# Encoder layer on one core: first MLP operands built inside the loop, last group added to the rows directly, row sums of the last chunk made later

## Chip, cores and metric

One core of a Trainium2 chip runs the whole program. The metric is the device time of one execution in microseconds. Engines are named as in the profile: PE (TensorE), DVE (VectorE), ACT (ScalarE), POOL (GpSimd), SP (SyncE, which only issues transfers here).

## What is computed

Two requests (2048 and 256 rows of width 1024) go through one layer: a normalised input projection, three mixers (windowed attention, a Fourier mix, attention into a memory), an output projection with a residual add, and a squared-ReLU MLP of width 4096 with a second residual add and a final norm. The change touches what begins at the output projection:

```python
x = x + group_output_norm(y_attn, y_four, y_mem, g_grp) @ w_out
hf = rmsnorm(x, g_ffn) @ w_ff1
x = x + jnp.square(jax.nn.relu(hf)) @ w_ff2
return rmsnorm(x, g_final)
```

## The kernel before

Rows are handled in 18 blocks of 128. Every fp32 operand of a product is split into a high part (ACT, `hi_of`) and a low part (`lo_of`, on DVE or POOL), and a product is three matmuls.

**Attention stage.** While attention runs, each finished block `b` goes through `outproj(b)`: a generator whose matmuls are drained a few at a time between attention's. It adds the projection to the rows `xr`, writes them to `X2d`, gets the row scale `xst` (squares on ACT, two small instructions on POOL), scales the rows (L845), transposes them in two halves (`xp`, PE) and multiplies by the gain (L855). `keep` (L861) then writes pieces of the result, `Xn`, that the MLP will read.

**MLP.** Rows are handled in three chunks of six blocks. Both products are done with seven half-size products instead of eight (a Strassen-like scheme), so sums and differences of the operands' quarters are needed. For the rows these are made block by block by POOL (L872): the second three blocks of a chunk are combined with the first three, which are fetched back from `XnT`. For chunk `c`, operand `i` of the rows is loaded as `XTl` (L991) and split by `build_x` into `XTh`, `XTl`.

One loop over `n` then interleaves, 14 steps apart, `product(n)` (first product: chunk, column pair `j`, operand `i` in the order `ORD1`) and `half_step(r)` (second product: chunk, group `g` of two column pairs, operand `i` in the order `ORD2`, half `e`). Weights are loaded in granules and split; in the first chunk the split first weights `w1s` (three buffers) are also written to `W1D` for the later chunks; for the second weights ACT makes `w2h` and POOL `w2l` (two buffers each). Each second product gathers in a PSUM tile `y` and DVE adds it to an accumulator `acc`, one per operand and block. After the last group of a chunk `finish(c, i)` combines the accumulators into the output rows (some sums on POOL, some on DVE), `measure` squares them (ACT), and `write` scales and stores them.

**Order.** The program is written in the order above, but a scheduler then orders the instructions of each engine; each engine runs its own list strictly in that order, and so does SP's queue of transfers. Before the loop the program writes the loads and the fourteen split pairs of the first chunk, drains the rest of the output projections of blocks 16 and 17, and frees their memory.

## Time and profile before

| | |
|---|---|
| median of 3 runs | 2377.63 us (2376.19 to 2380.34) |
| profiled execution | 2377.28 us, of which the span is 2375.5 us |
| busy | PE 2229.7 us (94%), DVE 1593.7 (67%), ACT 1003.9 (42%), POOL 1167.2 (49%) |
| chain that ended last | PE 52%, DVE 4%, POOL 3% of the span |

The share of PE is an average over stages. From about 380 to 852 us attention runs, from 922 to 2351 the MLP loop; PE's idle time lies mostly at the start, between these two stages, and at the end.

### The profile page before, as it was taken

How to read it: one execution, taken by the hardware profiler on the slowest of the kernel's cores; microseconds unless marked ns; L12 is line 12 of the kernel's file. 1: busy time of each engine (PE TensorE's matmuls, PEld its weight loads, DVE VectorE, ACT ScalarE, POOL GpSimd, SP SyncE). 2: the span in 40 equal slices, each digit the busy share in tenths (PEclk: the TensorE clock that was granted, in tenths of full speed). 3: DMA queues.
4: the chain of work that ended last, by engine and by line, in shares of the span. 5: the costliest groups of instructions: out<-in, count | busy, mean ns of one | idle time of the engine just before them, and what ended most of it. 6: DMA issues, size and time to landing. Idle time of an engine off the chain costs nothing.

```text
span 2375.5 us, 35784 instructions
## 1 busy us (share of the span) xinstructions
PE 2229.7 (94%) x12464; PEld 2004.1 (84%) x12464; DVE 1593.7 (67%) x2760; ACT 1003.9 (42%) x2353; POOL 1167.2 (49%) x1074
## 2 busy tenths in 40 slices
PE   7999996999998968999999999999999999999994
PEld 7999995887887857899999888999998889999983
DVE  6333477777676765888999986555557765555566
ACT  6332367665665643544444434222224332222233
POOL 3563031124123254877777575444444755444458
PEclk9999998999999988999999999999999999999997
DMA  8986257335444367666666867555557675555542
GB/s 295 322 286 236 93 157 284 128 130 167 150 149 146 125 234 267 243 224 221 226 225 223 314 203 259 193 192 186 188 193 271 205 243 189 192 187 188 195 155 84
DMA packets 187915, 484.89 MB, mean 204 GB/s; under 512 B 19607, under 2 KB 43159, under 8 KB 185431
## 3 DMA queue, kind: packets, MB, share of 16 engines
q1 hardware_dynamic: 168848, 427.20, 53.2%
q0 software_dynamic: 11696, 45.76, 5.7%
q10 hardware_dynamic: 7191, 9.65, 1.2%
q8 instruction: 99, 1.62, 0.3%
q14 instruction: 81, 0.66, 0.1%
HBM read 340.19 MB, written 143.26 MB: 204 GB/s over the span
## 4 chain that ended last, share of the span: by engine, by line
PE 52%; DVE 4%; POOL 3%; issue 1%; DMA 1%; ACT 0%; SPq 0%; POOLq 0%; ACTq 0%; DVEq 0%
PE y L100 26%; PE pc L100 8%; PE pb L100 7%; PE pa L100 7%; PE pd L100 4%; DVE acc L323 1%; POOL w2l L106 1%; DVE XTl L106 1%; DMA w1s<-W1D 0%; DVE al L106 0%; DVE x L323 0%; POOL ms L983 0%; DMA XTl<-Xn 0%; DVE m L323 0%; DVE acc L1194 0%
## 5 line engine op out<-in xcount | busy, mean ns | idle before, releaser
L106 POOL TENSOR_TENSOR w2l<-w,w2h 128x512 fp32r<-128x512 f32 x336 | 476.0, 1418 | 530.8 <-ACT w2h L103 520.5
L100 PE MATMUL y<-w2l,ah 128*128 128x512 f32 x1008 | 397.7, 394 | 13.7 <-POOL w2l L106 13.7
L100 PE MATMUL y<-w2h,al 128*128 128x512 f32 x1008 | 396.9, 395 | 0.0
L100 PE MATMUL y<-w2h,ah 128*128 128x512 f32 x1008 | 374.7, 395 | 6.1 <-DVE acc L323 4.3
L103 ACT ACTIVATE ah<-m 128x384 fp32r<-128x384 f32 x240 | 125.4, 524 | 471.7 <-PE y L100 453.8
L106 DVE TENSOR_TENSOR al<-m,ah 128x384 fp32r<-128x384 f32 x240 | 174.8, 729 | 157.7 <-ACT ah L103 154.3
L323 DVE TENSOR_TENSOR acc<-acc,y 128x512 f32<-128x512 f32 x396 | 255.5, 679 | 28.0 <-PE y L100 25.1
L100 PEld LDWEIGHTS y<-w2l,ah 128*128 128x128 f32 x1008 | 190.2, 189 | 42.3 <-POOL w2l L106 19.9
L100 PE MATMUL pc<-XTh,w1s 128*128 128x384 f32 x768 | 218.7, 339 | 6.9 <-DMA w1s<-W1D 3.2
L100 PEld LDWEIGHTS y<-w2h,ah 128*128 128x128 f32 x1008 | 189.3, 188 | 36.2 <-DVE acc L323 8.8
L100 PEld LDWEIGHTS y<-w2h,al 128*128 128x128 f32 x1008 | 190.1, 189 | 34.4
L100 PE MATMUL pb<-XTh,w1s 128*128 128x384 f32 x768 | 215.8, 337 | 1.5 <-ACT w1s L103 1.5
L100 PE MATMUL pa<-XTh,w1s 128*128 128x384 f32 x768 | 214.7, 338 | 2.0 <-ACT m L1085 1.1
L103 ACT ACTIVATE w2h<-w 128x512 fp32r<-128x512 f32 x336 | 207.2, 617 | 9.9 <-POOL w2l L106 4.4
L100 PE MATMUL pj<-hl_x,winh 128*128 128x256 f32 x720 | 206.6, 289 | 0.0
L100 PE MATMUL pj<-hh_x,winl 128*128 128x256 f32 x720 | 205.6, 287 | 0.0
L100 PE MATMUL pj<-hh_x,winh 128*128 128x256 f32 x720 | 204.1, 289 | 1.3 <-ACT hh_x L103 1.3
L1064 DVE SCALAR_TENSOR_TENSOR m<-m 128x384 f32<-128x384 f32 x192 | 175.5, 914 | 40.6 <-ACT m L1091 37.2
L100 PEld LDWEIGHTS pc<-XTh,w1s 128*128 128x128 f32 x768 | 142.6, 189 | 17.0 <-DVE m L323 3.3
L103 ACT ACTIVATE ah<-ms 128x384 fp32r<-128x384 f32 x96 | 50.5, 526 | 249.5 <-PE y L100 149.4
L100 PEld LDWEIGHTS pa<-XTh,w1s 128*128 128x128 f32 x768 | 142.2, 189 | 9.9 <-ACT m L1085 1.5
L100 PEld LDWEIGHTS pb<-XTh,w1s 128*128 128x128 f32 x768 | 141.9, 189 | 9.2 <-ACT w1s L103 1.9
(234 smaller groups left out, 5249.3 us busy)
## 6 DMA issues: line engine op xcount, KB each, us to landing
w1s<-W1D SPq DMA_DIRECT2D x224, 512.0 KB, 3.5
W1D<-w1s SPq DMA_DIRECT2D x112, 512.0 KB, 4.0
w<-in_w_dram SPq DMA_DIRECT2D x208, 256.0 KB, 3.9
w<-W2T SPq DMA_DIRECT2D x192, 256.0 KB, 3.7
w2r<-in_w_dram SPq DMA_DIRECT2D x16, 1024.0 KB, 7.3
W2T<-w2r POOLq DMA_DIRECT2D x16, 1024.0 KB, 6.2
XTl<-Xn SPq DMA_DIRECT2D x21, 768.0 KB, 8.1
qb<-Qd SPq DMA_DIRECT2D x18, 768.0 KB, 6.9
```

The source lines that it names most:

```text
L100: pe.matmul(out, lhsT, rhs, start=start, stop=stop, skip_group_check=more)
L103: act.activation(out, src, AF.Copy, scale=scale)
L106: (eng or dve).tensor_tensor(out=out, in0=src, in1=hi.bitcast(F32), op=ALU.subtract)
L323: TT(out=o, in0=a, in1=b, op=ALU.add)
L1064: dve.scalar_tensor_tensor(out=r, in0=r, scalar=0.0, in1=r, op0=ALU.max, op1=ALU.mult)
```

## The change

1. `outproj` scales each half of the rows by itself before its transposes, and takes the transposes' PSUM tile always from the same one-buffer pool. `keep` writes by SP's queue instead of POOL's, except for the four sums.
2. For the last chunk `outproj` makes no sums: it writes the second blocks to `XnT`, and a new `late_rows(t)`, called three times in the loop's second chunk, loads four pieces, makes the four sums on POOL and writes them.
3. Blocks 16 and 17 are drained before the MLP's operands are loaded in the program's text; only operands 1 and 6 are built before the loop, the other five in its first five steps, two ahead of their products.
4. `ORD2` runs operand 4 later (1, 2, 5, 6, 7, 4, 3). In the last chunk `finish` combines the accumulators one group earlier, and the last group uses `last_half_step`: products that go to the same rows gather in one PSUM tile, and each result is added to the rows directly.
5. In the last writes ACT scales the half whose gain POOL has multiplied already.

```diff
             rstd_of_means(st)
-            dve.tensor_scalar(out=xt, in0=xt, scalar1=st[:, 0:1], scalar2=None, op0=ALU.mult)
             xv = xt.rearrange("p (n t) -> p n t", n=2)
             for n in range(2):
...
+                dve.tensor_scalar(out=xv[:, n], in0=xv[:, n], scalar1=st[:, 0:1], scalar2=None, op0=ALU.mult)
+                ps = ps_p.tile([P, 4, P], F32, tag="p", name=f"xp_{b}_{n}")
...
-            def keep(i, v):
-                pool.dma_start(Xn[c, i][:, :, r * P:(r + 1) * P], v.rearrange("p (k t) -> p k t", k=KT // 2))
+            def keep(i, v, eng=sp):
+                eng.dma_start(Xn[c, i][:, :, r * P:(r + 1) * P], v.rearrange("p (k t) -> p k t", k=KT // 2))
...
+                if c == NCH - 1:
+                    sp.dma_start(XnT[b], xt)
+                else:
...
-        ORD2 = (1, 2, 4, 5, 6, 7, 3)
+        ORD2 = (1, 2, 5, 6, 7, 4, 3)
...
+        def last_half_step(r):
...
+                if e == 1:
+                    if i == 1 or i == 2:
+                        add(A(2, t), A(2, t), ps)
+                    elif i == 5:
+                        add(A("x", t), A("x", t), ps)
+                    elif i == 6 or i == 3:
+                        add(A(3, t), A(3, t), ps)
+                    elif i == 7:
+                        add(A("x", t), A("x", t), ps)
+                        add(A(4, t), A(4, t), ps)
+                    else:
+                        sub(A(4, t), A(4, t), ps)
...
+            if last_group(c, g):
+                for t in range(NT):
+                    if i == 2:
+                        measure(c, t, 0, A(2, t))
+                        ptt(A(2, t), A(2, t), acc[c, "g"][0], ALU.mult)
...
+        def late_rows(t):
+            a, b = (XnT[(NCH - 1) * CT + o + t].rearrange("p (n t) -> p n t", n=2) for o in (0, NT))
+            g = [granule(f"xl{i}_{t}", s) for i, s in enumerate((a[:, 0], a[:, 1], b[:, 0], b[:, 1]))]
+            for i, o in row_sums(*g):
+                sp.dma_start(Xn[NCH - 1, i][:, :, t * P:(t + 1) * P], o.rearrange("p (k t) -> p k t", k=KH))
...
-        for n, i in enumerate(ORD1):
-            for k in (0, 2):
-                drain(8)
-                build_x(0, i, k)
...
         drain(10 ** 9)
...
+        for n in range(2):
+            for k in (0, 2):
+                build_x(0, ORD1[n], k)
+            operand1(n)
...
+            if 2 <= n + 2 < 7:
+                for k in (0, 2):
+                    build_x(0, ORD1[n + 2], k)
+            if n >= PER + 40 and (n - PER - 40) % 8 == 0 and (n - PER - 40) // 8 < NT:
+                late_rows((n - PER - 40) // 8)
...
-                if g == NG - 1 and e == 1:
-                    pending += finish(c, i)
+                if g >= NG - 1 - (c == NCH - 1) and e == 1:
+                    pending += finish(c, g, i)
```

How the scheduler then orders the engines, at the three places that matter below. First DVE at the passage to the MLP, before the change (block 16's rows are `xr_9965`, block 17's `xr_10279`):

```order
L106 TENSOR_TENSOR XTl_0_10245<-XTl_0_10245,XTh_0_10244 128x768 x2
L323 TENSOR_TENSOR xr_10279<-xr_10279,op_1_10313 128x512
L106 TENSOR_TENSOR XTl_0_10248<-XTl_0_10248,XTh_0_10247 128x768 x2
L106 TENSOR_TENSOR XTl_0_10251<-XTl_0_10251,XTh_0_10250 128x768 x2
L106 TENSOR_TENSOR XTl_0_10254<-XTl_0_10254,XTh_0_10253 128x768 x2
L106 TENSOR_TENSOR XTl_0_10257<-XTl_0_10257,XTh_0_10256 128x768 x2
L106 TENSOR_TENSOR XTl_0_10260<-XTl_0_10260,XTh_0_10259 128x768 x2
L106 TENSOR_TENSOR XTl_0_10263<-XTl_0_10263,XTh_0_10262 128x768 x2
L845 TENSOR_SCALAR xr_10279<-xr_10279,xst_10355 128x1024
L855 TENSOR_TENSOR xr_10279<-xp_0_10363,gain 128x512
L855 TENSOR_TENSOR xr_10279<-xp_1_10369,gain 128x512
```

All seven split pairs stand here, block 17's second residual add behind the first of them and its scaling (L845) behind the last. After the change (block 16 is `xr_9972`, block 17 `xr_10249`):

```order
L323 TENSOR_TENSOR xr_10249<-xr_10249,op_0_10251 128x512
L106 TENSOR_TENSOR XTl_0_10356<-XTl_0_10356,XTh_0_10355 128x768 x2
L106 TENSOR_TENSOR XTl_0_10359<-XTl_0_10359,XTh_0_10358 128x768 x2
L323 TENSOR_TENSOR xr_10249<-xr_10249,op_1_10277 128x512
L106 TENSOR_TENSOR XTl_0_10362<-XTl_0_10362,XTh_0_10361 128x768 x2
L106 TENSOR_TENSOR XTl_0_10365<-XTl_0_10365,XTh_0_10364 128x768 x2
L106 TENSOR_TENSOR XTl_0_10368<-XTl_0_10368,XTh_0_10367 128x768 x2
L106 TENSOR_TENSOR w1s_0_7_10426<-w_0_2_10343,w1s_0_7_10426 128x512
L853 TENSOR_SCALAR xr_9972<-xr_9972,xst_10110 128x512 x2
L858 TENSOR_TENSOR xr_9972<-xp_0_10118,gain 128x512
L106 TENSOR_TENSOR w1s_0_5_10450<-w1s_0_10370,w1s_0_5_10450 128x512
```

Two pairs stand further ahead, not shown. The splits still stand ahead of the scaling, and now block 16's scaling (L853, two halves) is behind them as well; the two residual adds of block 17 stand between the splits. On PE at the same place, before:

```order
L100 MATMUL op_1_10313<-wol_4464,yth_1_10097 128x512
L100 MATMUL op_1_10313<-woh_4463,ytl_1_10098 128x512
L853 MATMUL xp_0_10363<-ident,xr_10279 128x128 x4
L853 MATMUL xp_1_10369<-ident,xr_10279 128x128 x4
L100 MATMUL pa_0_10432<-XTh_0_10244,w1s_0_1_10347 128x384
L100 MATMUL pa_0_10432<-XTl_0_10245,w1s_0_1_10347 128x384
```

Block 17's transposes `xp` follow its last output matmul, and the MLP's first product `pa` stands behind them. After:

```order
L100 MATMUL pb_0_10430<-XTh_0_10352,w1s_0_6_10387 128x384 x2
L100 MATMUL pb_0_10430<-XTl_0_10353,w1s_0_6_10387 128x384
L100 MATMUL pb_0_10430<-XTh_0_10352,w1s_0_6_10387 128x384
L856 MATMUL xp_0_10118<-ident,xr_9972 128x128 x4
L856 MATMUL xp_1_10125<-ident,xr_9972 128x128 x4
L100 MATMUL pc_0_10504<-XTh_0_10361,w1s_0_5_10450 128x384
```

The first two products of the MLP (`pa`, not shown, and `pb`) now stand ahead of block 16's transposes, and block 17's follow one product later. Last, POOL in the last group, before (`acc` and `x` rows are sums of accumulators):

```order
L106 TENSOR_TENSOR w2l_7_2_1_24214<-w_2_7_2_1_24153,w2h_7_2_1_24213 128x512
L106 TENSOR_TENSOR w2l_7_4_0_24236<-w_2_7_4_0_24189,w2h_7_4_0_24235 128x512
L983 TENSOR_TENSOR acc_2_0_20224<-acc_2_0_20224,acc_2_0_20362 128x512
L983 TENSOR_TENSOR acc_2_1_20226<-acc_2_1_20226,acc_2_1_20367 128x512
L106 TENSOR_TENSOR w2l_7_4_1_24261<-w_2_7_4_1_24211,w2h_7_4_1_24260 128x512
L983 TENSOR_TENSOR acc_2_2_20228<-acc_2_2_20228,acc_2_2_20372 128x512
L983 TENSOR_TENSOR ms_14_24243<-ms_14_24243,m_2_14_23746 128x384
L106 TENSOR_TENSOR w2l_7_5_0_24298<-w_2_7_5_0_24233,w2h_7_5_0_24297 128x512
```

After:

```order
L106 TENSOR_TENSOR w2l_7_2_1_24286<-w_2_7_2_1_24219,w2h_7_2_1_24285 128x512
L987 TENSOR_TENSOR ms_14_24268<-ms_14_24268,m_2_14_23795 128x384
L987 TENSOR_TENSOR m_2_14_23835<-m_2_14_23835,ms_14_24268 128x384
L987 TENSOR_TENSOR acc_2_0_20263<-acc_2_0_20263,gf_2_24308 128x512
L987 TENSOR_TENSOR acc_2_1_20265<-acc_2_1_20265,gf_2_24308 128x512
L106 TENSOR_TENSOR w2l_7_5_0_24315<-w_2_7_5_0_24258,w2h_7_5_0_24314 128x512
L987 TENSOR_TENSOR ms_15_24293<-ms_15_24293,m_2_15_24078 128x384
L106 TENSOR_TENSOR w2l_7_5_1_24338<-w_2_7_5_1_24283,w2h_7_5_1_24337 128x512
```

The sums of accumulators are gone from the last group; between operand 2's and operand 5's `w2l` stand now, beside two sums of the operand (`ms`, `m`), two multiplications of rows by the final gain (`gf`), which wait for ACT's measuring of those rows.

## Rows read from the trace of the kernel before

**Rows 1.** PE, DVE, ACT and POOL by stage: each row is a stretch of the span in us, its length, then busy us of each engine with its number of instructions, the granted TensorE clock as a share of 2.4 GHz, the busy share of the DMA engines and GB/s. The stretches are the passage from attention to the MLP, the MLP's first chunk, the last group's second products, and what follows the last matmul.

```profile
852.00:922.00 70.00, 40.85 (x180) 34.99 (x179) 37.90 (x40) 21.21 (x36) 38.91 (x38) 0.78 0.74 268
922.00:1400.00 478.00, 473.21 (x2378) 428.45 (x2377) 418.68 (x530) 207.72 (x389) 335.45 (x238) 1.00 0.70 242
2310.00:2351.00 41.00, 34.44 (x126) 23.66 (x124) 26.90 (x36) 14.82 (x31) 38.56 (x30) 0.96 0.21 58
2351.00:2376.00 25.00, 0.26 (x2) 0.00 (x0) 18.51 (x21) 8.56 (x21) 15.94 (x17) 0.58 0.34 126
```

**Rows 2.** What TensorE waited for, whole span (total us, times, longest): the wait of the block transposes `xp` for the normalised rows `xr`.

```profile
PE xp L853 <- DVE xr L845: 29.4, 5, 22.9
```

**Rows 3.** The passage in order of time, engine by engine (start, us, engine, line, operation, xcount; in brackets the idle time before it and its releaser). First TensorE, from block 16's first output half to the first of the MLP's second products (`y`).

```profile
852.25 0.39 PE L100 MATMUL op<-woh,ytl 128*128 128x512 f32 x1
871.98 0.39 PE L100 MATMUL op<-woh,ytl 128*128 128x512 f32 x1
895.30 1.94 PE L853 MATMUL xp<-ident,xr 128*128 128x128 f32 x8 [22.93 <-DVE xr L845]
898.11 0.66 PE L100 MATMUL pa<-XTh,w1s 128*128 128x384 f32 x1 [0.88 <-DVE xr L855]
911.14 0.69 PE L100 MATMUL pd<-XTh,w1s 128*128 128x384 f32 x1 [2.33 <-ACT w1s L103]
918.41 0.33 PE L100 MATMUL pb<-XTh,w1s 128*128 128x384 f32 x1
920.49 0.33 PE L100 MATMUL pa<-XTh,w1s 128*128 128x384 f32 x1
922.57 0.84 PE L100 MATMUL y<-w2h,ah 128*128 128x512 f32 x3
```

**Rows 4.** The same stretch on VectorE: block 17's second residual add, twelve of the fourteen splits of the first chunk's operands, and block 17's scaling.

```profile
877.48 0.67 DVE L323 TENSOR_TENSOR xr<-xr,op 128x512 f32<-128x512 f32 x1
878.07 14.99 DVE L106 TENSOR_TENSOR XTl<-XTl,XTh 128x768 fp32r<-128x768 f32 x12
892.99 2.16 DVE L845 TENSOR_SCALAR xr<-xr,xst 128x1024 f32<-128x1024 f32 x1
```

**Rows 5.** The same stretch on GpSimd (the power that ends block 17's row scale) and on SyncE's queue (issue of the seven operand loads).

```profile
882.05 1.30 POOL L138 TENSOR_TENSOR xst<-xst,mhalf 128x1 f32<-128x1 f32 x1
864.19 4.60 SPq L991 DMA_DIRECT2D XTl<-Xn  x7
```

**Rows 6.** The instructions on the operand tiles `XTl`, whole span (ns: min/median/max, then first and last start): ScalarE's high part and VectorE's low part.

```profile
L103 ACT ACTIVATE XTh<-XTl x42: 825/830/850, 872.3 to 1838.8; 128x768 fp32r<-128x768 f32 x42
L106 DVE TENSOR_TENSOR XTl<-XTl,XTh x42: 943/950/2242, 874.5 to 1843.6; 128x768 fp32r<-128x768 f32 x42
```

**Rows 7.** Two stretches of 2 us after the long wait, columns as in rows 1.

```profile
912.00:914.00 2.00, 2.00 (x8) 2.00 (x8) 0.00 (x0) 0.00 (x0) 0.00 (x0) 0.50 1.03 348
914.00:916.00 2.00, 1.05 (x5) 0.73 (x3) 0.20 (x1) 0.86 (x2) 0.00 (x0) 0.88 0.50 156
```

**Rows 8.** The end of the first chunk, 20 us stretches, columns as in rows 1; and GpSimd's subtractions that make the row sums, whole span (ns: min/median/max).

```profile
1380.00:1400.00 20.00, 20.00 (x104) 18.24 (x103) 16.10 (x22) 5.69 (x11) 16.64 (x13) 1.00 0.64 204
1400.00:1420.00 20.00, 18.49 (x93) 16.24 (x91) 17.02 (x21) 7.91 (x20) 14.45 (x12) 1.00 0.77 245
1420.00:1440.00 20.00, 16.96 (x81) 14.37 (x81) 20.00 (x25) 7.24 (x18) 17.44 (x18) 1.00 0.77 241
L872 POOL TENSOR_TENSOR xq<-xr,xq x18: 1272/1336/1986, 521.5 to 909.0; 128x512 f32<-128x512 f32 x18
```

**Rows 9.** The last group. GpSimd by line and operation from 2310 to 2351 (xcount, busy us, mean ns of one, idle before), and what TensorE waited for from 2310 on.

```profile
L106 POOL TENSOR_TENSOR w2l<-w,w2h 128x512 fp32r<-128x512 f32 x13 | 18.9, 1456 | 2.4 <-ACT w2h L103 2.4
L983 POOL TENSOR_TENSOR acc<-acc,acc 128x512 f32<-128x512 f32 x8 | 11.7, 1475 | 0.0
L983 POOL TENSOR_TENSOR x<-x,acc 128x512 f32<-128x512 f32 x3 | 4.1, 1390 | 0.0
PE y L100 <- POOL w2l L106: 5.3, 6, 1.3
PE y L100 <- ACT w2h L103: 0.9, 4, 0.3
```

**Rows 10.** The tail in order of time: TensorE's last matmul, four VectorE rows behind it, ScalarE's last instruction.

```profile
2350.87 0.39 PE L100 MATMUL y<-w2h,al 128*128 128x512 f32 x1
2357.26 0.68 DVE L323 TENSOR_TENSOR x<-x,acc 128x512 f32<-128x512 f32 x1
2362.66 1.75 DVE L1194 SCALAR_TENSOR_TENSOR x<-x,ff,gf 128x512 f32<-128x512 f32 x1
2365.59 0.74 DVE L1194 SCALAR_TENSOR_TENSOR x<-x,ff,gf 128x512 f32<-128x512 f32 x1
2370.35 0.75 DVE L1194 SCALAR_TENSOR_TENSOR acc<-acc,ff,gf 128x512 f32<-128x512 f32 x1 [0.84 <-POOL ff L138]
2371.57 0.72 ACT L1192 ACTIVATE acc<-fg,ff 128x512 f32<-128x512 f32 x1 [3.16 <-DVE acc L1194]
```

**Rows 11.** What SyncE's queue waited for, whole span (total us, times, longest), the two rows of the loads of the residual rows `xr`; and who waited for writers of `xr` between 380 and 920.

```profile
SPq L819 <- DMA Xn<-xq: 68.5, 8, 14.0
SPq L819 <- DMA XnT<-xr: 62.0, 5, 16.3
  POOL Xn L861: 36.3, 34
```

More of the change, by code (lines that the diff above doesn't have):

```diff
@@ L814, in open_out, with row_sums @@
                 scaled_split(*wo[k], s, gain[:, 2, k:k + 1])
+        def row_sums(b11, b21, b12, b22):
+            for o, u, v, i in ((b11, b12, b11, 5), (b12, b22, b12, 7), (b22, b22, b11, 6), (b21, b22, b21, 4)):
+                pool.tensor_tensor(out=o, in0=u, in1=v, op=ALU.subtract)
+                yield i, o
         def outproj(B):
@@ L1150, in load_acc, with last_group, multiply @@
                         sp.dma_start(acc[c, i, t], X2d[b][:, n * 512:(n + 1) * 512])
+        def last_group(c, g):
+            return c == NCH - 1 and g == NG - 1
+        def multiply(ps, k, t, start, stop, more=False):
+            ah, al = opsA[k]
+            wh, wl = ops2[k]
+            ts_ = slice(t * P, (t + 1) * P)
+            mm(ps, ah[:, ts_], wh, start, False, more)
+            mm(ps, ah[:, ts_], wl, False, False, more)
+            mm(ps, al[:, ts_], wh, False, stop, more)
         def half_step(r):
             c, g, i, e = steps2[r]
-            ah, al = opsA.pop(steps2[r])
-            wh, wl = ops2.pop(steps2[r])
             for t in range(NT):
@@ L1188, in write @@
                 o = hv[n]
-                if end and n == 1:
-                    t = granule(f"fg_{b}", None)
-                    pool.tensor_tensor(out=t, in0=o, in1=gf[n], op=ALU.mult)
-                    act.activation(o, t, AF.Copy, scale=st[:, 0:1])
+                if end and n == 0:
+                    act.activation(o, o, AF.Copy, scale=st[:, 0:1])
                 else:
@@ L1232, in trunk @@
[L1232 to L1242 removed]
+            if i == 1 and g == NG - 1:
+                acc[c, "g"] = gains_of(c)
+            if last_group(c, g):
+                for t in range(NT):
+                    if i == 2:
+                        measure(c, t, 0, A(2, t))
+                        ptt(A(2, t), A(2, t), acc[c, "g"][0], ALU.mult)
+                    elif i == 7:
+                        measure(c, NT + t, 1, A("x", t))
+                    elif i == 4:
+                        measure(c, NT + t, 0, A(4, t))
+            else:
+                for t in range(NT):
+                    if i == 1:
+                        acc[c, "x", t] = granule(f"x22_{c}_{t}", X2d[c * CT + NT + t][:, 512:1024])
+                    elif i == 2:
+                        ptt(A(2, t), A(2, t), A(1, t), ALU.add)
+                    elif i == 5:
+                        ptt(A("x", t), A("x", t), A(5, t), ALU.add)
+                    elif i == 6:
+                        ptt(A(6, t), A(6, t), A(1, t), ALU.add)
+                    elif i == 7:
+                        add(A(7, t), A(7, t), A(6, t))
+                        ptt(A(6, t), A(6, t), A(5, t), ALU.add)
+                        add(A("x", t), A("x", t), A(7, t))
+                    elif i == 4:
+                        add(A(4, t), A(4, t), A(7, t))
+                    elif i == 3:
+                        add(A(3, t), A(3, t), A(6, t))
+                    if not last:
+                        for o, h, k in ((2, 0, 2), (7, 1, "x"), (4, 1, 4), (3, 0, 3)):
+                            if i == o:
+                                measure(c, h * NT + t, 1 if k in ("x", 3) else 0, A(k, t))
@@ new lines, in finish @@
+            if g == NG - 1 and i == 4:
+                return [lambda t=t: write(c, NT + t, [A(4, t), A("x", t)], acc[c, "g"]) for t in range(NT)]
+            if g == NG - 1 and i == 3 and not last:
+                return [lambda t=t: write(c, t, [A(2, t), A(3, t)], acc[c, "g"]) for t in range(NT)]
+            return []
+        def late_rows(t):
[3 more added lines that the diff above has]
+                sp.dma_start(Xn[NCH - 1, i][:, :, t * P:(t + 1) * P], o.rearrange("p (k t) -> p k t", k=KH))
@@ L1246, in trunk @@
         rp = region(right, "right", "ffn_r")
+        ps_y = region(right, "right", "ps_fy", 1, PSUM)
         ps_h = region(right, "right", "ps_fh", 1, PSUM)
-        ps_y = region(right, "right", "ps_fy", 1, PSUM)
+        w1_first(0)
+        for i in ORD1:
+            load_x(0, i)
+        w1_sums(0, 0)
+        for n in range(2):
+            for k in (0, 2):
+                build_x(0, ORD1[n], k)
+            operand1(n)
         w1_first(1)
```

80 lines of the change are left out of this document (27 added, 53 removed).

## Prediction

> **What bounds the kernel now.** I read the stages first, then the waits of TensorE, then the two places where the stages lose time. In the first chunk of the MLP PE is busy 473.2 of 478 us [rows 1]: there, time is saved only by less matmul work, and the change takes none away. The passage from attention to the MLP is another matter: PE works 40.9 of 70 us, at a mean clock of 0.78. Behind the last matmul 24 us pass without PE, and in the last group PE works 34.4 of 41 us while POOL is busy 38.6 [rows 1]. So the three places hold some 29, 24 and 7 us of idle PE, and a low clock beside.
>
> The list of waits names the first: of 29.4 us in which transposes `xp` waited for scaled rows, 22.9 are one wait [rows 2]. In order of time the reader sees it whole: PE ends block 17's output product at 872, starts its transposes at 895.3, and the MLP's first product `pa` stands in the queue behind them until 898.1 [rows 3]. The row scale was there at 883.4, but DVE was in the middle of twelve splits in a row and took up the scaling only at 893.0 [rows 4, 5]. PE was not waiting for the MLP's data; it was waiting, in its fixed order, for an instruction behind other work on DVE.
>
> **The passage (-22 us).** By the order of the changed program PE goes from block 17's output product straight to `pa` and `pb`, with block 16's transposes behind these. PE reached the end of that product at 872 with block 16's transposes (8, under 1 us) already done, so in the new order it gets there near 871. `pa` can start then if its operands are split. The operand loads were issued at 864.2 behind block 16's rows [rows 5]; in the new order they stand ahead of these in SP's queue, so I take them as there. That would be 27 us earlier than 898.1, the upper end.
>
> But the splits are not moved out of the way. DVE's new list has three pairs behind block 17's second add, and block 16's scaling behind these. From the add, which ends near 872: six splits at between 0.95 [rows 6] and 1.25 us (14.99 over 12, rows 4), say 6.4; one low part of a weight and a half scaling, about 1.1. So block 16's transposes start near 879.5. PE has `pa` and `pb` until then, 2.08 us each at full clock (918.41 to 920.49, rows 3), that is until 875.2: a new wait of 4 to 5 us takes the place of the 22.9.
>
> From there to the first second product `y` PE has 16 transposes (2 us), five products (10.4), two waits of about 1.5 for the second halves, since the transposes now share one PSUM buffer, and the wait for weights that it has now (2.33 before `pd`, rows 3), because the three `w1s` buffers turn no faster. That is 18 us at full clock. After a wait of 2.33 us the clock stood at 0.50 for 2 us and at 0.88 for the next 2 [rows 7], at 0.5 of 2.4 GHz the lower level, 1.2 GHz; I put 2 to 3 us on that. `y` then starts near 900 instead of 922.6: -22. Lower bound: if all five products run at 1.2 GHz, 10 us more, -12. Upper: -27.
>
> **The row sums of the last chunk (+4 us).** Twelve subtractions leave this passage, where POOL had them on the way to the row scale, and turn up, by POOL's order, at the end of the first chunk and the start of the second. At 1.34 us each [rows 8] they are 16.1 us of POOL. The three stretches there have POOL busy 48.5 of 60, and PE idle in the last two (1.5 and 3.0 us, rows 8): 16.1 go into 11.5 free, so 4.6 push `w2l` back, and PE with it. Bounds 0 (spread wider) and 16.1. Their 24 transfers lie on a queue whose DMA engines are at 0.64 to 0.77 there; I give them nothing.
>
> DVE is busy 53.1 of the same 60 us, 20 of the last 20 [rows 8]. A DVE instruction with two operands took 0.74 or 1.75 us in the tail, the longer one while POOL ran [rows 10]; 12 times the difference is 12 us, below the upper bound.
> The Trainium skill speaks against the move here: "SBUF — State Buffer", section "Who interferes with whom", has a DVE instruction with two SBUF inputs and a GpSimd instruction that reads SBUF exclude each other for a whole instruction. By that rule each of the twelve can cost DVE its length, which would make this term +12 rather than +4.
>
> **The last group (-2 us).** Eleven sums of accumulators, 15.8 us of POOL, go [rows 9]; they are made one group earlier, where PE has first products to run beside. PE waited 6.2 us for split weights here, and the mean clock was 0.96 of 41 us, 1.6 us [rows 1, 9]. But the two multiplications by the gain now stand ahead of operand 5's `w2l`, and wait for ACT's measuring. From the last matmul of block 1's rows: an add 0.68, the measuring about 0.7, two multiplications and one `w2l` at 1.46 to 1.48: 5.8 us, against nine matmuls, 2.1 us. That is a wait of 3.7, and the third multiplication gives one of about 1.5. So 7.8 becomes some 5.5. Bounds -6.5 (POOL keeps ahead) and +3.
>
> **The tail (-12.7 us).** Behind its last matmul, which ends at 2351.3, the old program has DVE adds of accumulators until 2357.9 and later, nine scalings, some of them stretched from 0.74 to 1.75 us by POOL's work, and ends with ACT at 2372.3, 3.2 us before the end of the span [rows 10]. In the new one DVE has three adds (0.68) and nine scalings (0.74) left, 8.7 us, about 8 since neighbours overlap, with nothing large on POOL; the scales for the first are made while PE ends. With 0.3 us behind them and the same 3.2 us for the transfer: 11.5 instead of 24.2. Bounds -10 (four instructions stretched by 1 us, start half a microsecond late) and -14.5.
>
> **Attention (-2 us).** The other four waits for the scaling are 6.5 us [rows 2]; with halves of half the length, and POOL rid of 51 issues of transfers (counted in the code; 39 go to SP, twelve of the rest to the later sums), I take a third of it. Bounds -6.5 and +9. The other order of `ORD2` changes no count of anything; its operand 5 has its sums one to two steps earlier, and I see no wait there: 0.
>
> **Sum.** 2377.3 (profiled execution; 0.35 below the median) - 22 + 4 - 2 - 12.7 - 2 = 2342.6, on the median 2343.
>
> **Rivals.**
> 1. *The wait stays on DVE* (2353 to 2372, 0.20). The splits are still ahead of the scaling, and if one runs at its longest, 2.24 us [rows 6], or the loads come as late as now (issued at 864), `pa` itself waits and block 16's transposes start near 890. Then the passage gives 10 instead of 22, and with +8 for the row sums the time is 2359. For it: DVE's order. Against: SP's order. (If only DVE is held up by the twelve subtractions, +12 instead of +4, the time is 2351, inside the forecast.)
> 2. *More is won* (below 2331, 0.10). No wait at `xp` (-27), the sums hidden (0), the last group free of waits (-6.5): 2329.
> 3. *SP's queue holds attention back* (0.06). It now carries the 39 writes of normalised rows, and each waits for DVE in front of the loads of the next queries. POOL waited 36.3 us for such rows [rows 11]. If 35 us of these waits reach PE, about 2.2 for each of 16 blocks, all is lost; at 50, 2392, slower. It decides where a load lands after PE has ended the block before it. Against it: the queue stood 68.5 and 62.0 us behind loads that waited for POOL's writes [rows 11], and these get shorter.
> 4. *Nothing moves* (0.02): each wait reappears as another at the same place, 2376.
>
> **How the numbers follow.** The forecast (2331 to 2352) has 0.62. Within 0.2%, 4.8 us, a measurement of this kernel cannot tell a change. Faster by more: the forecast, rivals 1 and 2, 0.92. Same: rival 4 and a third of rival 3, 0.04. Slower: the rest of rival 3, 0.04. The range 2328 to 2366 takes in the forecast, half of rival 2 and some two thirds of rival 1, 0.8.
>
> **What would show it.** Between the end of block 17's output product and `y` there should be 26 to 30 us instead of 50, with one wait of 4 to 5 us at `xp` and its releaser the scaling in halves. The part behind the last matmul should be 11 to 13 us, and the last DVE scaling 4 us or less before the end. In the last group a wait of `y` for `w2h` or `w2l` right behind operand 2. At the first chunk's end POOL over 90% busy. It is wrong if `pa` waits for `XTh` or `w1s` at 871, if attention's stretch gets longer by more than 5 us, or if the end of chunk 1 loses more than 16.

## The result, and the profile after

The changed kernel takes 2342.98 us (median of 4 runs, 2337.87 to 2346.21) against 2376.91 of the kernel before on the same chip: ratio 0.9859 (95% interval 0.9843 to 0.9875), 33.5 us less by the ratio. The forecast was 2343. The total came out; several of its terms did not, and the reason given for the largest does not suffice by itself.

Both traces can be cut at the same matmuls: the first scores of attention, the last matmul of block 17's output product, and each 126th second product (a group has 126). Lengths in us, from their start times, in the profiled execution of each kernel (2377.28 and 2344.84 us):

| stretch | before | after | difference |
|---|---|---|---|
| start, to the first scores | 369.6 | 371.7 | +2.1 |
| attention, to the end of block 17's output product | 502.4 | 492.7 | -9.7 |
| passage, to the first `y` | 50.6 | 27.9 | -22.7 |
| first chunk, groups 1 to 6 | 370.6 | 369.3 | -1.3 |
| end of the first chunk: its groups 7, 8 and the next chunk's first | 189.8 | 196.6 | +6.7 |
| from there to the last chunk's group 7 | 770.6 | 769.6 | -1.0 |
| last chunk, group 7 | 56.2 | 62.2 | +6.0 |
| last chunk, group 8 (the last) | 41.1 | 40.2 | -0.9 |
| tail, from the start of the last matmul | 24.6 | 13.0 | -11.7 |
| span | 2375.5 | 2343.0 | -32.5 |

The edit does not touch the start, and its length varies from 366 to 372 in the profiles of this study.

The stages of the changed kernel, in the columns of [rows 1]: passage, groups 1 to 6, end of the first chunk, then the last chunk's groups 7 and 8 and the tail.

```profile
864.40:892.30 27.90, 20.75 (x103) 18.45 (x101) 16.72 (x25) 9.82 (x19) 12.26 (x7) 0.88 0.82 286
892.30:1261.60 369.30, 368.17 (x1862) 334.94 (x1863) 313.94 (x415) 159.58 (x301) 264.90 (x187) 1.00 0.70 239
1261.60:1458.20 196.60, 183.73 (x883) 162.33 (x883) 160.91 (x199) 79.78 (x157) 143.27 (x108) 0.97 0.81 278
2227.70:2289.90 62.20, 58.04 (x285) 51.76 (x283) 43.48 (x60) 15.62 (x31) 43.57 (x34) 0.97 0.45 148
2289.90:2330.40 40.50, 33.29 (x127) 23.68 (x125) 29.99 (x41) 19.23 (x43) 32.66 (x28) 0.96 0.21 59
2330.40:2343.00 12.60, 0.02 (x1) 0.00 (x0) 7.21 (x12) 4.23 (x9) 5.58 (x8) 0.71 0.67 250
```

The same end of the first chunk, and group 7 of the last, in the kernel before:

```profile
1293.20:1483.00 189.80, 180.45 (x883) 160.91 (x881) 153.77 (x199) 79.35 (x157) 123.36 (x96) 0.98 0.76 256
2253.60:2309.80 56.20, 56.20 (x284) 50.96 (x284) 32.41 (x51) 15.61 (x31) 29.15 (x25) 1.00 0.50 164
```

Group 7 of the last chunk, full before, now holds 4.2 us of idle PE; at the end of the first chunk idle PE grows from 9.4 to 12.9 us. The rest of what the two stretches lose, 1.8 and 3.3 us, is PE busy for longer, at a mean clock of 0.97 instead of 1.00 and 0.98. The loss of the first chunk's end lies in group 8, 76.9 us instead of 62.7; the group behind it is 5.7 shorter.

The passage of the changed kernel on TensorE, answering [rows 3]:

```profile
864.38 0.39 PE L100 MATMUL op<-woh,ytl 128*128 128x512 f32 x1
864.61 0.34 PE L100 MATMUL pa<-XTh,w1s 128*128 128x384 f32 x1
871.81 1.11 PE L856 MATMUL xp<-ident,xr 128*128 128x128 f32 x4 [2.87 <-DVE xr L853]
873.71 1.12 PE L856 MATMUL xp<-ident,xr 128*128 128x128 f32 x4 [0.78 <-DVE xr L858]
881.77 0.62 PE L100 MATMUL pd<-XTh,w1s 128*128 128x384 f32 x2 [1.04 <-DVE w1s L106]
892.27 0.97 PE L100 MATMUL y<-w2h,ah 128*128 128x512 f32 x3 [0.94 <-ACT ah L103]
```

`pa` follows the output product at once. The new wait at `xp` is 2.87 us where the prediction had 4 to 5, its releaser is the scaling in halves (L853), and the waits for the second halves of blocks 16 and 17 are 0.78 each instead of 1.5.

The tail, answering [rows 10]: the last matmul, the first of DVE's last three adds, and the last scalings of ACT and DVE.

```profile
2330.03 0.39 PE L100 MATMUL yl<-w2h,al 128*128 128x512 f32 x1
2331.02 0.67 DVE L323 TENSOR_TENSOR acc<-acc,yl 128x512 f32<-128x512 f32 x1
2337.63 0.72 ACT L1233 ACTIVATE acc<-acc,ff 128x512 f32<-128x512 f32 x1 [0.91 <-POOL ff L138]
2337.63 0.75 DVE L1235 SCALAR_TENSOR_TENSOR acc<-acc,ff,gf 128x512 f32<-128x512 f32 x1 [0.77 <-POOL ff L138]
```

The arithmetic ends 8 us behind the last matmul, as worked out; 4.6 us of transfer follow instead of 3.2.

### The profile page after: what moved, and what is told of

Read it like the earlier page. It is cut to its first block, busy times and chain, and to the rows that moved or that the text cites. A ratio compares the mean times of both kernels' runs of the same rounds, so it can differ in the third digit from the quotient of the medians.

```text
span 2343.0 us, 35879 instructions
## 1 busy us (share of the span) xinstructions
PE 2229.2 (95%) x12464; PEld 2005.2 (86%) x12464; DVE 1561.4 (67%) x2781; ACT 1003.4 (43%) x2353; POOL 1139.7 (49%) x1023
## 3 DMA queue, kind: packets, MB, share of 16 engines
q1 hardware_dynamic: 192896, 446.86, 56.2%
## 4 chain that ended last, share of the span: by engine, by line
PE 67%; DVE 8%; DMA 4%; ACT 2%; issue 2%; POOL 1%; SPq 0%; POOLq 0%; ACTq 0%; DVEq 0%
PE y L100 26%; PE op L100 8%; PE pc L100 8%; PE pb L100 8%; PE pa L100 8%; PE pd L100 4%; DMA X2d<-xr 1%; DVE acc L323 1%; PE s L100 1%; PE ot L100 1%; PE t L687 1%; DVE p L661 1%; DMA XTl<-Xn 1%; DVE al L106 1%; PE otm L100 1%
## 5 line engine op out<-in xcount | busy, mean ns | idle before, releaser
L106 POOL TENSOR_TENSOR w2l<-w,w2h 128x512 fp32r<-128x512 f32 x336 | 484.3, 1443 | 494.8 <-ACT w2h L103 490.2
L100 PE MATMUL y<-w2l,ah 128*128 128x512 f32 x966 | 380.9, 395 | 6.4 <-POOL w2l L106 6.4
L100 PE MATMUL y<-w2h,al 128*128 128x512 f32 x966 | 381.9, 396 | 0.0
L100 PE MATMUL y<-w2h,ah 128*128 128x512 f32 x966 | 360.7, 398 | 17.6 <-DVE acc L323 9.0
L106 DVE TENSOR_TENSOR al<-m,ah 128x384 fp32r<-128x384 f32 x240 | 182.9, 763 | 180.2 <-ACT ah L103 167.6
L323 DVE TENSOR_TENSOR acc<-acc,y 128x512 f32<-128x512 f32 x378 | 244.3, 680 | 24.1 <-PE y L100 20.0
L100 PEld LDWEIGHTS y<-w2h,al 128*128 128x128 f32 x966 | 183.3, 190 | 33.1
L100 PEld LDWEIGHTS y<-w2l,ah 128*128 128x128 f32 x966 | 183.3, 190 | 30.4 <-POOL w2l L106 7.8
L1068 DVE SCALAR_TENSOR_TENSOR m<-m 128x384 f32<-128x384 f32 x192 | 159.0, 828 | 42.5 <-ACT m L1095 39.0
L100 PEld LDWEIGHTS pj<-hl_x,winh 128*128 128x128 f32 x720 | 139.3, 194 | 1.3 <-DVE hl_x L106 1.2
```

Of the source, the lines that this page charges most:

```text
L100: pe.matmul(out, lhsT, rhs, start=start, stop=stop, skip_group_check=more)
L106: (eng or dve).tensor_tensor(out=out, in0=src, in1=hi.bitcast(F32), op=ALU.subtract)
L323: TT(out=o, in0=a, in1=b, op=ALU.add)
L1068: dve.scalar_tensor_tensor(out=r, in0=r, scalar=0.0, in1=r, op0=ALU.max, op1=ALU.mult)
```

## The experiments

Each kernel was timed against the kernel before on the same chip, so ratios are compared. The changed kernel's is 0.9859; 0.001 is 2.4 us. The stretches, cut as above ("chunk end" is the end of the first chunk). They come from one profiled execution of each kernel, which lies up to 6 us from the median of its runs (start only, sums back, GpSimd queue and neither 5 to 6 us below it); attention takes 490.4 to 493.6 us in all kernels with its new length, so 3 us there mean little:

| kernel | attention | passage | groups 1-6 | chunk end | group 7 | group 8 | tail |
|---|---|---|---|---|---|---|---|
| before | 502.4 | 50.6 | 370.6 | 189.8 | 56.2 | 41.1 | 24.6 |
| after | 492.7 | 27.9 | 369.3 | 196.6 | 62.2 | 40.2 | 13.0 |
| start only | 501.6 | 42.2 | 376.6 | 188.9 | 56.2 | 41.1 | 24.5 |
| sums back | 493.1 | 47.4 | 373.8 | 185.8 | 63.5 | 39.1 | 13.1 |
| buffer held | 490.9 | 43.4 | 377.3 | 197.0 | 62.3 | 40.1 | 13.0 |
| all built | 492.1 | 27.1 | 369.2 | 198.0 | 63.2 | 39.2 | 13.0 |
| sums quiet | 490.7 | 27.3 | 370.0 | 188.9 | 63.3 | 39.2 | 13.0 |
| one column | 490.9 | 26.9 | 370.0 | 192.1 | 63.7 | 39.1 | 13.0 |
| last undone | 490.8 | 26.2 | 369.7 | 196.8 | 56.2 | 49.7 | 17.2 |
| quiet, fix | 491.4 | 26.6 | 369.6 | 188.6 | 61.5 | 38.2 | 13.0 |
| GpSimd queue | 493.6 | 32.0 | 372.5 | 197.6 | 62.4 | 39.9 | 13.3 |
| whole rows | 490.4 | 27.9 | 369.1 | 195.9 | 63.3 | 39.1 | 13.0 |
| neither | 500.9 | 29.3 | 372.6 | 198.0 | 62.3 | 40.1 | 13.3 |

**Start only.** The kernel before with the third part of the change and, of the first, the one-buffer pool of the transposes.

```diff
+        drain(10 ** 9)
...
+        for i in ORD1:
+            load_x(0, i)
...
+        for n in range(2):
+            for k in (0, 2):
+                build_x(0, ORD1[n], k)
...
+            if 2 <= n + 2 < 7:
...
```

> The kernel before with the third part of the change alone: blocks 16 and 17 drained ahead of the operand loads in the text, two operands built before the loop and five in it, the transposes always in the same one-buffer pool. Scaling of whole rows, GpSimd's queue for the normalised rows, row sums and last group are as before. Theory: the order of the start alone takes the wait of 22.9 us away: 18 to 23 us less than the kernel before, 2354 to 2359. Rival: it takes the scaling in halves, SyncE's queue and GpSimd free of the sums as well; alone it gives 8 to 13 us, 2364 to 2369.

Measured: 2377.4, ratio 0.9989 (0.9977 to 1.0002): nothing that can be told from the kernel before. Both expectations fall. `pa` came 26 us earlier, but then PE waits elsewhere:

```profile
889.60 0.69 PE L100 MATMUL pc<-XTh,w1s 128*128 128x384 f32 x1 [8.27 <-ACT w1s L103]
911.86 0.48 PE L100 MATMUL pa<-XTh,w1s 128*128 128x384 f32 x1 [4.69 <-ACT w1s L103]
916.10 0.79 PE L100 MATMUL y<-w2l,ah 128*128 128x512 f32 x1 [2.81 <-POOL w2l L106]
```

The weights are late. The passage gives 8.4 and the groups behind it take 6.0 back, in a profiled execution of 2371.5, itself 6 us below the median.

**Sums back.** The changed kernel, with the last chunk's row sums in the output projection.

```diff
-                if c == NCH - 1:
-                    sp.dma_start(XnT[b], xt)
-                else:
+                if True:
...
-                late_rows((n - PER - 40) // 8)
```

> The changed kernel with the row sums of the last chunk back in the output projection, as in the other chunks, everything else as changed. Theory: the passage did not need them gone, since GpSimd is busy only 19.5 of its 48 us; the end of the first chunk gets its 6.7 us back and the passage loses 0 to 3: 2337 to 2340. Rival: the sums stand in GpSimd's list ahead of the row scale of block 17 and of the first weight sums, and VectorE's splits of 0.95 us get longer beside them; then the passage loses 8 to 16 us and the time is 2345 to 2352.

Measured: 2357.5, ratio 0.9910 (0.9894 to 0.9927), 12 us above the changed kernel: the rival, and beyond its 2345 to 2352. The chunk end gains 10.8, passage and first groups lose 24. So most of the passage's gain hangs on the sums being gone. GpSimd's time there need not be the reason: its first weight sum waits for the load of the weights,

```profile
855.65 1.29 POOL L985 TENSOR_TENSOR w1s<-w,w 128x512 f32<-128x512 f32 x1 [5.87 <-DMA w<-in_w_dram]
```

and SyncE's queue shows why that comes late. Its rows where it issues the load of block 17's rows (and, where they follow, the first weights), in the kernel before,

```profile
859.89 0.33 SPq L819 DMA_DIRECT2D xr<-in_x_dram  x1
860.79 3.36 SPq L893 DMA_DIRECT2D w<-in_w_dram  x4
```

and what the queue waited for there (waits that reach into 845 to 862, counted whole),

```profile
SPq L819 <- DMA Xn<-xq: 20.4, 2, 11.0
```

with the sums back in the changed kernel,

```profile
847.36 0.34 SPq L825 DMA_DIRECT2D xr<-in_x_dram  x1
848.23 3.33 SPq L895 DMA_DIRECT2D w<-in_w_dram  x4
```

and in the changed kernel:

```profile
821.54 0.33 SPq L825 DMA_DIRECT2D xr<-in_x_dram  x1
842.85 2.59 SPq L897 DMA_DIRECT2D w<-in_w_dram  x4
```

The sums fetch the partner rows into `xq`, which takes one of the three buffers of the rows (tag `xr`). The load of block 17's rows waits until block 15's sums are written out, and weights and operands of the MLP stand behind it in the queue. The wait was in [rows 11], 68.5 us in all.

**Buffer held.** To tell the buffer from the arithmetic. (The fetches into it and the writes that release it come with it; `Xs` is the scratch area.)

```diff
...
                 if c == NCH - 1:
                     sp.dma_start(XnT[b], xt)
+                    x1 = op.tile([P, 2, 512], F32, tag="xr", bufs=3, name=f"xq_{b}")
+                    pool.dma_start(x1.rearrange("p n t -> p (n t)"), XnT[b - NT])
+                    v = [x1[:, 0], x1[:, 1], xv[:, 0], xv[:, 1]]
+                    full = {5: v[0], 7: v[2], 6: v[3], 4: v[1]}
+                    for i, o in row_sums(*(q[:, 0:1] for q in v)):
+                        pool.dma_start(Xs[r, i], full[i])
```

> The changed kernel, in which blocks 15 to 17 take, beside everything that they do now, the third buffer of the rows as the old sums did: the first blocks' rows are fetched into it, the four subtractions run on one column instead of 512, and the pieces are written to a scratch area that nobody reads. The real sums stay in the second chunk. So the buffer is held as long as before, and GpSimd has next to no arithmetic more. Theory: the passage was late because SyncE's load of block 17's rows waited for that buffer, and the loads of the MLP's weights stand behind it in the queue; with the buffer held the weights come late again, and 15 to 23 us of the passage are lost: 2357 to 2366 where the changed kernel has 2343. Rival: it was the time of the subtractions on GpSimd, 16 us, and what they do to VectorE's splits; then within 4 us of the changed kernel, 2342 to 2347.

Measured: 2363.3, ratio 0.9944 (0.9931 to 0.9958), 20 us above the changed kernel with next to no arithmetic more: the theory by time, but only in part by the route that it names. SyncE's queue waited for the scratch writes, and issued the rows and, behind them, three of the seven operand loads late:

```profile
SPq L826 <- DMA Xs<-xq: 10.5, 1, 10.5
```

```profile
854.27 0.33 SPq L826 DMA_DIRECT2D xr<-in_x_dram  x1
854.70 1.97 SPq L1002 DMA_DIRECT2D XTl<-Xn  x3
```

But the first weights and four operands were issued ahead of them, at 839 to 844. What stood longest in front of the splits was GpSimd's own list: it waited 7.13 us at the fetch of the next partner rows, which waits for these writes as well, and the sums of the first weights stand behind that fetch. ScalarE waited for these sums, VectorE for ScalarE, and the splits stand behind that in VectorE's list:

```profile
852.90 0.54 POOL L875 DMA_DIRECT2D xq<-XnT  x1 [7.13 <-DMA Xs<-xr]
856.16 0.63 ACT L103 ACTIVATE w1s<-w1s 128x512 fp32r<-128x512 f32 x1 [7.97 <-POOL w1s L994]
856.82 1.10 DVE L106 TENSOR_TENSOR w1s<-w1s,w1s 128x512 fp32r<-128x512 f32 x1 [6.12 <-ACT w1s L103]
858.69 7.27 DVE L106 TENSOR_TENSOR XTl<-XTl,XTh 128x768 fp32r<-128x768 f32 x7 [0.17 <-ACT XTh L103]
876.32 1.12 PE L857 MATMUL xp<-ident,xr 128*128 128x128 f32 x4 [11.29 <-DVE xr L854]
```

The splits begin 1.8 us ahead of the start of the output product's last matmul; in the changed kernel it is 8.2. That is 6.4 of the 8.4 us by which the wait at `xp` has grown. So the held buffer costs the time, through two lists that run in order; how much goes by SyncE's and how much by GpSimd's in the kernel before is not told apart.

**All built.** All operands built ahead of the loop in the text.

```diff
-        for n in range(2):
+        for n in range(7):
             for k in (0, 2):
                 build_x(0, ORD1[n], k)
-            operand1(n)
+            if n < 2:
+                operand1(n)
...
-            if 2 <= n + 2 < 7:
-                for k in (0, 2):
-                    build_x(0, ORD1[n + 2], k)
```

> The changed kernel with all seven operands built ahead of the loop in the text, as before the change, instead of two there and five in the first steps of the loop; the output projections are still drained first. VectorE's list at the passage is nearly the same in both: all splits ahead of block 16's scaling. Theory: where the text builds them makes no difference, within 3 us of the changed kernel, ratio 0.985 to 0.987. Rival: the few weight splits that change places with them are waited for, 3 to 8 us more.

Measured: 2342.1, ratio 0.9841 (0.9828 to 0.9855), somewhat under the expected 0.985 to 0.987, but the intervals overlap: not to be told from the changed kernel. The part that stands first in the title does nothing by itself: the scheduler lays VectorE's splits in the same order either way.

**Sums quiet.** The late sums in the middle of the second chunk.

```diff
-            if n >= PER + 40 and (n - PER - 40) % 8 == 0 and (n - PER - 40) // 8 < NT:
-                late_rows((n - PER - 40) // 8)
...
+                if r > PER + 30 and (r - PER - 30) % 8 == 7 and (r - PER - 30) // 8 < NT:
+                    late_rows((r - PER - 30) // 8, acc[c, i, 0])
...
+                act.activation(g[i], after, AF.Copy)
                 sp.dma_start(g[i], s)
```

> The changed kernel with the row sums of the last chunk made in the quiet middle of the second chunk (groups 2 to 4 of 8). They are held there by a copy on ScalarE into each of the twelve tiles, which reads an accumulator of that step, before the tile is loaded; the twelve copies are extra work of about 0.6 us each on an engine that is 43% busy. Theory: the 6.7 us that the change loses between the start of the first chunk's last groups and the second group of the second chunk come from these twelve subtractions, because VectorE's two-operand adds take 1.5 to 2.0 us instead of 0.7 while one runs and the PSUM tiles of the second products come free late. In the middle of the chunk TensorE has no idle time, so they are hidden: 5 to 7 us less than the changed kernel, 2336 to 2338. Rival 1: the loss there comes from the other order of the operands and the sums of accumulators that follow it: within 1.5 us of the changed kernel, 2342 to 2345. Rival 2: the subtractions cost VectorE their length wherever they lie, and the loss moves with them: also 2342 to 2345, but with new waits of y in groups 2 to 4.

Measured: 2334.7, ratio 0.9814 (0.9798 to 0.9831), 10.7 us under the changed kernel, more than expected; the chunk end gives 7.7 of it, and 2.0 lie in attention, which this edit does not touch. The end of the first chunk, and the twelve subtractions, of this kernel:

```profile
1259.90:1448.80 188.90, 180.16 (x886) 161.89 (x886) 152.76 (x199) 80.48 (x158) 125.69 (x96) 0.98 0.73 244
```

```profile
L819 POOL TENSOR_TENSOR xl<-xl,xl x12: 1281/1392/1609, 1552.3 to 1629.6; 128x512 f32<-128x512 f32 x12
```

From 1459 to 1740 this kernel's TensorE waited for nothing, so the loss does not move with the sums; both rivals fall. In the text of the changed kernel the call stands in the second chunk as well; but the pieces use the buffers of the first chunk's weights, and as soon as those are free the scheduler puts the sums there, 1313 to 1390. A true dependency (the copy of an accumulator) held them.

What they cost in the changed kernel is read from VectorE between 1316 and 1392:

```profile
L106 DVE TENSOR_TENSOR al<-m,ah 128x384 fp32r<-128x384 f32 x11 | 13.0, 1186 | 2.9 <-ACT ah L103 2.9
L323 DVE TENSOR_TENSOR acc<-acc,y 128x512 f32<-128x512 f32 x18 | 11.7, 678 | 1.3 <-PE y L100 1.2
L323 DVE TENSOR_TENSOR x<-x,acc 128x512 f32<-128x512 f32 x3 | 4.8, 1616 | 0.0
L106 DVE TENSOR_TENSOR al<-ms,ah 128x384 fp32r<-128x384 f32 x4 | 3.5, 873 | 2.1 <-ACT ah L103 2.1
```

and from TensorE's waits from 1261 to 1459:

```profile
PE y L100 <- DVE acc L323: 7.7, 6, 3.8
PE y L100 <- DVE acc L326: 3.3, 1, 3.3
PE y L100 <- POOL w2l L106: 1.3, 2, 0.9
```

With the sums away, the same window has

```profile
L106 DVE TENSOR_TENSOR al<-m,ah 128x384 fp32r<-128x384 f32 x12 | 10.0, 833 | 3.4 <-ACT ah L103 3.4
L323 DVE TENSOR_TENSOR x<-x,acc 128x512 f32<-128x512 f32 x3 | 3.7, 1256 | 0.0
L106 DVE TENSOR_TENSOR al<-ms,ah 128x384 fp32r<-128x384 f32 x4 | 4.6, 1141 | 2.4 <-ACT ah L103 2.4
```

With the sums there, the splits `al<-m` take 1186 ns on average instead of 833 and the adds of two SBUF operands 1616 instead of 1256; the adds with a PSUM operand take 678 in both. Not every form is longer: the four splits `al<-ms` take 873 with the sums and 1141 without; GpSimd is busy 55 of these 76 us without them too (66 with them). Over the whole chunk end VectorE is busy 160.9 us with the sums there and 152.8 without. PE hardly waits for `w2l` (1.3 us), as the prediction had it, but for PSUM tiles that a delayed VectorE gives back late (11.0). The contrast between one and two SBUF operands agrees with the Trainium skill, "SBUF — State Buffer", section "Who interferes with whom": a VectorE instruction with at most one SBUF input, outside its two-port modes, does not contend with GpSimd; one with two contends with a GpSimd instruction that reads SBUF.

**One column.** The late subtractions on one column, at their places, all transfers kept.

```diff
+            full = {5: g[0], 7: g[2], 6: g[3], 4: g[1]}
-            for i, o in row_sums(*g):
+            for i, _ in row_sums(*(q[:, 0:1] for q in g)):
...
```

> The changed kernel with the twelve late subtractions on one column instead of 512, at the same places of GpSimd's order, with all 24 transfers as they are; so the last chunk's sums are left out of the computation, and the time is that of a kernel without their arithmetic. Theory: the loss at the end of the first chunk is the arithmetic (GpSimd's 16 us, and VectorE's two-operand instructions that take twice as long beside it), so it goes as it did when the sums were moved: ratio 0.981 to 0.983, 7 to 11 us under the changed kernel. Rival: it is the transfers and the nine buffers that the pieces share with the weights: ratio within 0.0015 of the changed kernel's 0.9859.

Measured: 2338.6, ratio 0.9829 (0.9811 to 0.9848), 7 us under the changed kernel, as the theory had it, though the two intervals just overlap. The chunk end is 192.1: by it, 4.5 us were the arithmetic. The other 3.2 that moving the sums gives would fall to what stays here, the 24 transfers, the buffers and twelve short instructions; these were not told apart.

**Last undone.** The changed kernel with the old last group.

```diff
         def last_group(c, g):
-            return c == NCH - 1 and g == NG - 1
+            return False
...
-                if g >= NG - 1 - (c == NCH - 1) and e == 1:
+                if g == NG - 1 and e == 1:
...
```

> The changed kernel with the last group as it was: every chunk combines its accumulators behind its own last group, no direct adds to the rows, the old last writes; the new order of the operands stays. Theory, from the two traces: the tail behind the last matmul goes from 12.6 back to 24 us, and the 5 us that the change loses in the last two groups come back: 6 to 8 us more than the changed kernel, 2349 to 2351. Rival, the prediction's own sum (tail 12.7, last group 2): 14 to 15 us more, 2357 to 2358.

Measured: 2348.5, ratio 0.9871 (0.9854 to 0.9888), 2.9 us above the changed kernel by the ratios, whose intervals overlap, and 7.8 by the three last columns of the table (-6.0, +9.6, +4.2), where the theory had 6 to 8. Not the 14 of the prediction's sum. The old last group with the new order of operands has a tail of 17.2, not 24.6, but takes 8.6 us longer itself: 66.9 for both, against 65.7. The waits of TensorE in the changed kernel's groups 7 and 8:

```profile
PE yl L100 <- POOL w2l L106: 5.1, 5, 1.7
PE y L100 <- POOL w2l L106: 2.2, 1, 2.2
PE y L100 <- DVE acc L326: 2.0, 1, 2.0
PE yl L100 <- DVE acc L323: 1.9, 1, 1.9
```

The two waits of `y` are in group 7, which is back at its old 56.2 here: the sums of accumulators, one group earlier, are not hidden by the first products there.

**Quiet, fix.** The kernel with the quiet sums, and one sum of the last chunk written otherwise.

```diff
                     elif i == 6:
                         ptt(A(6, t), A(6, t), A(1, t), ALU.add)
+                        if last:
+                            ptt(A(5, t), A(5, t), A(6, t), ALU.add)
                     elif i == 7:
                         add(A(7, t), A(7, t), A(6, t))
-                        ptt(A(6, t), A(6, t), A(5, t), ALU.add)
+                        if not last:
+                            ptt(A(6, t), A(6, t), A(5, t), ALU.add)
...
-                        add(A(3, t), A(3, t), A(6, t))
+                        add(A(3, t), A(3, t), A(5 if last else 6, t))
```

> The kernel with the row sums in the quiet middle of the second chunk (2334.7 in its own comparison, 0.9814 of before), and in the last chunk one sum of accumulators written otherwise: GpSimd adds operand 6's accumulator to operand 5's behind operand 6, instead of operand 5's to operand 6's behind operand 7, where it must wait for VectorE to read the old value. Theory: the last chunk's last but one group loses 6 us because GpSimd stands behind those three sums with the next split weights (waits of y of 2.2 for w2l and 2.0 for an accumulator, and a low clock behind them); with the sums earlier 3 to 5 us come back: ratio 0.979 to 0.980. Rival: VectorE is the bound there, with three operands' adds and twelve sums of accumulators in one group, and the wait for it grows by what the other gives: within 1 us, 0.981 to 0.982.

Measured: 2329.9, ratio 0.9806 (0.9790 to 0.9822): faster than both kernels, but not to be told from the quiet sums alone by time. Groups 7 and 8 are 2.8 us shorter in the trace; the two waits of 2.2 and 2.0 have become one, for VectorE:

```profile
PE y L100 <- DVE acc L326: 3.5, 1, 3.5
```

So it lies between the two expectations: the wait for GpSimd is gone, the one for VectorE has grown from 2.0 to 3.5.

**GpSimd queue.** All transfers of normalised rows back on GpSimd's queue.

```diff
-            def keep(i, v, eng=sp):
+            def keep(i, v, eng=pool):
...
-                sp.dma_start(XnT[b], xt)
+                pool.dma_start(XnT[b], xt)
```

> The changed kernel with all transfers of normalised rows back on GpSimd's queue. Theory, from the traces: attention is 9.7 us shorter in the changed kernel because GpSimd no longer issues and waits for them between the small instructions of the row scales and statistics; with them back 6 to 10 us are lost there: 2349 to 2353 where the changed kernel has 2343. Rival: the gain comes from the scaling in halves, which hides the queue either way: within 3 us, 2341 to 2346.

**Whole rows.** The rows scaled in one instruction again.

```diff
+            dve.tensor_scalar(out=xt, in0=xt, scalar1=st[:, 0:1], scalar2=None, op0=ALU.mult)
             for n in range(2):
-                dve.tensor_scalar(out=xv[:, n], in0=xv[:, n], scalar1=st[:, 0:1], scalar2=None, op0=ALU.mult)
```

> The changed kernel with the rows scaled in one instruction of 1024 columns again, everything else as changed. Theory, the same as for the run with GpSimd's queue: the queue is what attention gained by, so the halves are worth only half an instruction, 0.4 us, at each of the 18 blocks, most of it hidden: 0 to 3 us more than the changed kernel, 2343 to 2346. Rival: the halves are the gain: 6 to 10 us more, 2349 to 2353.

Measured: queue back 2354.7, ratio 0.9908 (0.9892 to 0.9925), 11.7 us above the changed kernel; whole rows 2341.4, ratio 0.9853 (0.9840 to 0.9867), no difference. Neither moves attention. With the queue back the loss lies behind it, in the passage (+4.1), the first groups (+3.2) and the chunk end (+1.0), where no expectation put it; what makes it was not settled. Both theories gave attention's gain to the queue; the queue alone does not make it.

**Neither.** Both edits together.

> The changed kernel with both small parts of the output projection undone: rows scaled in one instruction, and the normalised rows written by GpSimd's queue. With either of them undone alone, attention (from its first scores to the end of block 17's output product) kept its new length, 493.5 and 490.4 us where the changed kernel has 492.7 and the kernel before 502.4. Theory: either of the two is enough, since both shorten the same stretch between the row scale and the next block; without both, attention goes back to 500 to 503 us. Rival: neither makes it, it is the order in which the scheduler lays the rest, without the sums of blocks 15 to 17; then 489 to 495 us.

Measured: 2360.8, ratio 0.9920 (0.9907 to 0.9934), and attention back at 500.9: the theory. Its wait for scaled rows between 400 and 869 is near what it was in [rows 2] without the long one, 6.5:

```profile
PE xp L856 <- DVE xr L852: 7.6, 5, 4.7
```

In the changed kernel it is 1.4. Either edit keeps attention short; together they give no more than one.

## Why the prediction was right in the sum and wrong in its parts

- **Passage, -22: right in size** (-22.7), with nearly the shape described: 27.9 us from the end of the output product to `y`, one wait at `xp` released by the scaling. **The step that failed is its cause.** The prediction took the loads as there because they stand ahead of block 16's rows in SyncE's new order, and gave all the gain to that order. The order alone gives nothing by time: the weights come late (start only). The third buffer of the rows, which the moved sums no longer take, has to be free as well: held again, with its fetches and writes and next to no arithmetic, it costs 20 us (buffer held). The sums were charged +4 and credited with nothing here. The reverse, the sums moved under the old order, was not run, so whether the order is needed at all stays open.
- **Row sums, +4: too small.** +6.7 at the chunk end, where 7.7 come back when they are moved away (10.7 by time). With the sums back in the projection this stretch took 185.8, 4.0 less than in the kernel before, so the rest of the change may give something there and the sums cost up to 10.8; no run tells this apart. The route was wrong as well: PE waited 1.3 us for POOL's `w2l` there and 11.0 for VectorE's adds. That is the mechanism of the Trainium skill's rule that the prediction weighed; the +12 worked out from it is above every one of these figures.
- **Last group, -2: wrong in sign**, +5.0 with group 7. The sentence "where PE has first products to run beside" put the earlier sums at no cost; they cost 6.0. Within the last group the forecast was near (-0.9), and the wait that it named is there, at half its size: 1.73 us for `w2l` behind operand 2, where it had 3.7.
- **Tail, -12.7: right** (-11.7), apart from 1.4 us more of transfer. But 7.4 of it are there with the old last group too, under the new order of the operands, where the group itself takes 8.6 longer (last undone).
- **Attention, -2: too small.** -9.7, of which about 1 is block 16's transposes gone to the passage. The prediction took a third of the waits for scaling; 5.1 of these 6.5 us went. The rest was not taken apart.
- **Operand order, 0: not isolated by any run.** The end of the second chunk, where no row sums are made, takes 187.4 us instead of 188.5 (its groups 7 and 8 and the next chunk's first): in all, little changes there.

The errors cancel, so that the sum came this near is luck: attention -7.7, the sums +2.7, the last two groups +7.0, tail +1.0, passage -0.7, and the stretches that no term covers (start, groups 1 to 6, the end of the second chunk) -0.2. That makes -32.6 of the sum's -34.7; the spans differ by 32.5.

## What to carry to other kernels

When work is moved out of a stage, look at the buffers that it held and at who waits for them, not only at its engine time: here SyncE's queue, and in one run GpSimd's list, stood behind a transfer that wanted such a buffer. A place in the text does not place an instruction where a scheduler may move it; here a dependency did. And GpSimd's work on SBUF is best put where TensorE does not wait for VectorE.

## What the runs showed of the hardware

A one-column GpSimd instruction of the changed kernel, 0.30 us at the median of its eighteen, took 5.73 us while VectorE ran six splits, a weight split and the scaling without a pause, and ended with them:

```profile
865.46 5.29 DVE L106 TENSOR_TENSOR XTl<-XTl,XTh 128x768 fp32r<-128x768 f32 x6
871.28 0.87 DVE L853 TENSOR_SCALAR xr<-xr,xst 128x512 f32<-128x512 f32 x2
866.46 5.73 POOL L137 TENSOR_SCALAR xst<-xst 128x1 f32<-128x1 f32 x1 [8.15 <-ACT xjk L849]
```

With the start alone changed, one subtraction of weights beside such a run took 6.08 us instead of 1.3, and ended 1.1 us behind the run:

```profile
884.47 6.08 POOL L980 TENSOR_TENSOR w1s<-w,w 128x512 f32<-128x512 f32 x1 [3.21 <-DMA w<-in_w_dram]
```

So it seems that GpSimd can wait not for one VectorE instruction but for a whole run of them. It is not always so: in the kernel before, the same one-column instruction came through in the middle of twelve splits [rows 4],

```profile
879.59 1.68 POOL L137 TENSOR_SCALAR xst<-xst 128x1 f32<-128x1 f32 x1
```

and there the splits were the longer ones, 1.25 us each instead of 0.88. What decides between the two was not measured.
